# Gates of the GLA branch: from a plain product and a one-group unit to one seven-product unit of two groups

## The chip, the cores and the metric

The kernel runs on one core of a Trainium2 chip. The metric is the device time of one execution in microseconds (us), the median of several runs. The profile is that of one execution; TensorE is PE (its weight loads PEld), VectorE DVE, ScalarE ACT, GpSimd POOL, SyncE SP.

## The reference

The kernel computes one decoder layer in float32, for 512 tokens of width 1024. Only the token mixer matters here:

```
h = layer_norm(x)
q_g, k_g, v_g, r_g, a_lr, q_lat, kv_lat, gate_logits = split(h @ w_in)   # widths 512, 512, 1024, 1024, 16, 384, 320, 2048
o_gla = gla_chunked(q_g, k_g, v_g, log_sigmoid(a_lr @ w_gla_a2 + b) / 16)  # 4 heads
y_gla = (rms_norm(o_gla) * silu(r_g)) @ w_o_gla
y_mla = mla_attention(q_lat, kv_lat) @ w_o_mla
g_gla, g_mla = split(sigmoid(gate_logits + b_gate))                       # 1024 columns each
mix   = (g_gla * y_gla + g_mla * y_mla) @ w_out
h = layer_norm(alpha * h + mix);  out = layer_norm(alpha * h + square(relu(h @ w_ff1)) @ w_ff2)
```

The change concerns the product that makes the 1024 logits of g_gla, and work earlier in the kernel that prepares operands for it.

## The kernel before

**Products in three parts.** Each float32 operand is split into a high and a low half (`split`: ScalarE writes hi, L111, VectorE writes lo = x - hi, L112), and a product is three matmuls: hi by hi, hi by lo, lo by hi. In a product with the weights as the stationary operand these are L245, L246 and L247 (`gemm_fm`, moving tiles of 512 tokens); with the activations stationary, L279 to L281 (`gemm_tm`); in the product of r, L728 to L730 (`proj_r`); in the seven-product units, L1157 to L1159 (`unit`, moving tiles of 256 tokens). PSUM has two pools of four banks, pm (`MM`) and px (`PX`).

**Weights.** `plan` lists all weight tiles in the order of their use in one stream. `pump(i)` fetches two tiles ahead (on SP) and splits one tile ahead (hi on ScalarE at L189, lo on VectorE at L190), in three buffers of raw weights (wraw) and two each of hi and lo (whi, wlo).

**Seven products.** A product of 2 x 2 blocks is done with seven block products in place of eight, by Strassen's method in Winograd's form. Three of the products (11, 21, 22) use blocks of the weights as they are, and four (t1, t2, t3, t4) use sums of blocks: t1 is the load of block 12 on SP with an accumulating load of block 11 on POOL's queue (`u_load`, L1132 and L1134), t3 likewise with 22, and t2 and t4 follow from t1 and t2 by VectorE sums (`u_sum`, L356). The activations need the matching sums of h's blocks. `h_early` makes these for four pairs of k tiles: hraw (L1046) is hi plus lo of a tile again, hx (L1050 to L1053) are four sums and differences, and the halves of each are split into hs and written to DRAM as hsd (L1060). They are read back twice: by `proj_r` (xr) and, ahead of the gates, by `h_load` into sh (L1216). `proj_r` and three units use this form: g0 and g1 for the gates and f1 for a part of the first MLP product. A unit with two groups has two column groups of 512 output channels each, and so two sets of banks.

**The work around the change.** The product of q (from about 45 us) and of k are plain. Then come v of the first two heads, r, and v of the other two (to about 217 us), and beside them the decay levels of GLA: `gla_levels` copies the cumulated log decays of a head into rp (L766), POOL advances them by powers of two (L775, L776), ScalarE takes the exponentials E (L781), VectorE multiplies them by q and k into M (L783), and TensorE multiplies M by itself (L837, L841, L845). `gla_out` multiplies the scores by v (L880 to L882), squares (osq, L884), sums (gss, L887), takes the root on POOL (grs, L889), scales (og, L894) and transposes on TensorE (L900). From 217.90 us the gates of the first 512 channels of g_gla are a plain product (`gemm_fm` of `PL["g", 0]`), and then the other 512 channels are unit g0 with one group. Unit g1, with two groups, makes the 1024 channels of g_mla. Where a helper makes work in pieces, the pieces are co-routines: `spawn` puts one in a list, and `tick` lets the first few do a step each, between matmuls.

**The order.** The program is recorded in this way, and a scheduler then orders the instructions of each engine by a simulated timeline before the program runs. The order on each engine is fixed from then on. `tc.issue_after` holds one instruction behind another in it.

Of the kernel before, what the change touches and what calls it, by code (L numbers as in the profile page):

```python
# [52 lines left out]
def tile_hybrid_block(ctx: ExitStack, tc: tile.TileContext, I, out, dbg=None):  # L53
# [29 lines left out]
    def DR(shape, n):  # L83
        n = nm(n)
        return pd.tile(shape, F32, tag=n, name=n)
# [7 lines left out]
    def f(ap):  # L93
        return ap.bitcast(F32)
# [137 lines left out]
    def part(x, i, c):  # L232
        return x[i][:, c] if isinstance(x, tuple) else x[:, i, c]
# [94 lines left out]
    def plan_qr(g):  # L328
        PL["qr", g] = plan("w_q_b", NOPE, 4 * ROPE, heads=(HQ, 4 * g, 4))

    PL["g", 0] = plan("w_in", C_G, T)

    HOME = {"w": ("whi", "wlo"), "r": ("wraw", "wraw"), "a": ("xh", "xl")}
    FMO = (("11", 0), ("21", 1), ("t1", 2), ("22", 5), ("t2", 3), ("t3", 6), ("t4", 4))
    HELD = (("21", "f1"), ("21", "g0"), ("22", "g0"))
    ORDER = {"g0": ("11", "t1", "21", "t2", "22", "t3", "t4")}
    UNITS = {"g0": ("w_in", C_G + T, 1), "g1": ("w_in", C_G + D, 2), "f1": ("w_ff1", 3 * D, 2)}

    def plan_src(key, seq, homes):
        PL[key] = []  # L340
# [356 lines left out]
    def proj_r():  # L697
        bank, e, xs = {}, {}, {}

        def x_load(ph):  # L700
            xs[ph] = []
            for p in range(4):
                t = B([P, 2, 256], F32R, "xr")
                nc.sync.dma_start(f(t), hsd[p][(2, 3, 5, 6).index(ph)])
                xs[ph].append((t[:, 0], t[:, 1]))

        nat = {0: (0, 0), 1: (1, 0), 4: (1, 1)}
        for n, (op, ph) in enumerate(RW):
            if n + 1 < len(RW) and RW[n + 1][1] not in nat:
                x_load(RW[n + 1][1])  # L710
            if ph in nat:
                i, h = nat[ph]
                x = [tuple(hT[2 * p + i][:, w, 256 * h:256 * h + 256] for w in range(2)) for p in range(4)]
            else:
                x = xs.pop(ph)
            opens = ph in (0, 1, 2)
            for hf in range(2):
                it = PL["r"][2 * n + hf]
                pump(it)
                hi, lo = stream[it]["w"]  # L720
                for pp in range(2):
                    xh, xl = x[2 * hf + pp]
                    for t in range(2):
                        key = ("a" if ph in (0, 3, 6, 4) else "b", t)
                        if ph in (0, 1) and not hf and not pp:
                            bank[key] = MM()
                        o, c = bank[key], slice(t * P, (t + 1) * P)
                        mm(o, xh[:, c], hi[:, pp], start=opens and not hf and not pp, stop=False, skip_group_check=True)  # L728
                        mm(o, xh[:, c], lo[:, pp], start=False, stop=False, skip_group_check=True)
                        mm(o, xl[:, c], hi[:, pp], start=False, stop=hf == 1 and pp == 1, skip_group_check=True)  # L730
                    if (hf, pp) in RT:
                        tick(None)
            for t in range(2):
                a, b = bank["a", t], bank.get(("b", t))
                if ph in (0, 3, 2):
                    e[ph, t] = B([P, T], F32, "er")
                    act(e[ph, t], b if ph == 2 else a, AF.Copy)
                elif ph == 1:
                    vtt(e[0, t], b, e[0, t], op=ALU.add)
                    silu(0, t, e[0, t])  # L740
                elif ph == 6:
                    vtt(e[2, t], e[2, t], a, op=ALU.subtract)
                    silu(1, 2 + t, e[2, t])
                elif ph == 5:
                    vtt(e[3, t], b, e[3, t], op=ALU.subtract)
                    silu(1, t, e[3, t])
                else:
                    silu(0, 2 + t, a)
            if op == RA4:
                r_acc4()  # L750
# [11 lines left out]
    def gla_levels(h):  # L762
        qk = QK[h]
        QK[h] = None
        rp = A([P, 2, T], F32, "rp")
        nc.vector.tensor_copy(rp[:, 1, :], GL[h])  # L766
        nc.gpsimd.memset(rp[:, 0, :], 0.0)
        SD = B([P, NT, P], F32, "SD")
        SDf = SD.rearrange("p t i -> p (t i)")
# [267 lines left out]
    hsd = []  # L1037

    def h_early():
        for _ in range(6):  # L1040
            yield
        for p in range(4):
            raw = [B([P, T], F32, "hraw") for _ in range(2)]
            for i in range(2):
                h = hT[2 * p + i]
                vtt(raw[i], f(h[:, 0]), f(h[:, 1]), op=ALU.add)  # L1046
            yield
            a11, a12, a21, a22 = raw[0][:, :256], raw[1][:, :256], raw[0][:, 256:], raw[1][:, 256:]
            X = [B([P, 2, 256], F32, "hx") for _ in range(2)]
            vtt(X[0][:, 0], a21, a22, op=ALU.subtract)  # L1050
            vtt(X[0][:, 1], X[0][:, 0], a11, op=ALU.subtract)
            vtt(X[1][:, 0], a12, X[0][:, 1], op=ALU.add)
            vtt(X[1][:, 1], a11, a21, op=ALU.subtract)  # L1053
            yield
            hsd.append([DR([P, 2, 256], "hsd") for _ in range(4)])
            for i, x in enumerate(X):
                xs = [B([P, 2, 256], F32R, "hs") for _ in range(2)]
                for e in range(2):
                    split(x[:, e], xs[e][:, 0], xs[e][:, 1])
                    nc.sync.dma_start(hsd[p][2 * i + e], f(xs[e]))  # L1060
                yield

    t_ln1 = spawn(ln_in1())
# [72 lines left out]
    def unit(key, ops, evac, after=None, pb=None):  # L1136

        bank, e1, e5, u2 = {}, {}, {}, {}

        def prod(op):  # L1140
            ph = dict(FMO)[op]
            opens = ph in (0, 2, 1)
            for g in range(UNITS[key][2]):
                bk = ("a" if ph in (0, 3, 6, 4) else "b" if ph in (2, 5) else "c", g)
                if opens:
                    bank[bk] = (PX if ph == 1 else (pb or MM) if ph == 2 else MM)()
                o, it = bank[bk], PL[key, op, g]
                pump(it)
                hi, lo = stream[it]["w"]
                for k in range(4):  # L1150
                    while len(ops) <= k:
                        tick(3)
                    xh, xl = ops[k][ph]
                    for a in range(2):
                        c = slice(a * P, (a + 1) * P)
                        oa = o[:, a * 256:(a + 1) * 256]
                        mm(oa, hi[:, k, c], xh, start=opens and k == 0 and a == 0, stop=False, skip_group_check=True)  # L1157
                        mm(oa, hi[:, k, c], xl, start=False, stop=False, skip_group_check=True)  # L1158
                        mm(oa, lo[:, k, c], xh, start=False, stop=k == 3, skip_group_check=True)  # L1159
                    if k == 3 or k == 1 and key != "g0":  # L1160
                        tick(3)
                if ph == 0:
                    e1[g] = B([P, T], F32, "e1")
                    act(e1[g], o, AF.Copy)
                elif ph == 1:
                    vtt(e1[g], o, e1[g], op=ALU.add)
                    evac(0, 0, g, e1[g], True)
                elif ph == 2:
                    e5[g] = B([P, T], F32, "e5")
                    act(e5[g], o, AF.Copy)  # L1170
                elif ph == 3:
                    u2[g] = B([P, T], F32, "u2")
                    act(u2[g], o, AF.Copy)
                if ph == (5 if key == "g0" else 3):
                    vtt(u2[g], bank["b", g], u2[g], op=ALU.subtract)
                    evac(1, 0, g, u2[g], True)
                if ph == 6:
                    vtt(e5[g], e5[g], o, op=ALU.subtract)
                    evac(1, 1, g, e5[g], True)
                elif ph == 4:  # L1180
                    evac(0, 1, g, o, False)
            if after:
                after(op)
        return prod
# [17 lines left out]

    def ev_gate0(j, i, g, ps, _):
        for a in range(2):
            gate(0, 4 + 2 * j + a, ps[:, a * 256:(a + 1) * 256], slice(256 * i, 256 * i + 256))

    hops = []

    def h_load():
        for p in range(4):  # L1210
            o = {0: (0, 0), 1: (1, 0), 4: (1, 1)}
            o = {ph: tuple(part(hT[2 * p + i], w, slice(256 * h, 256 * h + 256)) for w in range(2))
                 for ph, (i, h) in o.items()}
            for x, ph in enumerate((2, 3, 5, 6)):
                t = B([P, 2, 256], F32R, "sh")
                nc.sync.dma_start(f(t), hsd[p][x])  # L1216
                o[ph] = (t[:, 0], t[:, 1])
            hops.append(o)
            yield

    spawn(h_load())
    u_load("g0", "t1")
    u_load("g0", "22")
    gemm_fm(PL["g", 0], hT, T, lambda a, ps: gate(0, a, ps, slice(0, T)))
    def after0(op):
        if op == "11":
            for o in ("t3", "21"):
# [400 lines left out]
```

## Time and profile before

| | |
|---|---|
| median of 3 runs | 891.93 us (891.44 to 892.49) |
| the profiled execution | 891.75 us, span 890.0 us |
| granted TensorE clock | 0.998 |
| PE busy | 871.3 us (98%) |
| PEld busy | 757.1 us (85%) |
| DVE busy | 634.6 us (71%) |
| ACT busy | 467.0 us (52%) |
| POOL busy | 186.8 us (21%) |

The span runs from the first to the last instruction of the profile, and the profiled execution's own time lies 1.75 us around it. Busy times count each engine's own instructions, and engines overlap. A matmul is drawn until its modelled end, so it overlaps its successor: the pitch from start to start tells its cost on TensorE. In timelines the columns are start, duration, engine, line, operation, output from inputs, sizes, and the number of instructions that are drawn together; a bracket gives idle time of the engine before the instruction and who ended it. In groups they are the count, busy time and mean in ns, and the idle time before. In rows of DMA the last number is the median time in us from issue to landing.

### The profile page before, as it was taken

To read this page: it belongs to the slowest core of one execution; us is meant where nothing else is said; L and a number is where in the kernel's file an instruction comes from. 1 tells how busy PE (TensorE), PEld (TensorE's weight loads), DVE (VectorE), ACT (ScalarE), POOL (GpSimd) and SP (SyncE) were. 2 spreads that over 40 slices of the span, in tenths; PEclk is the share of its full clock that TensorE was granted. 3 is DMA by queue.
4 is the path that set the end of the run, shared out by engine and by line. 5 is a ranking of instruction groups with operands and counts; after the bars stand their busy time and mean duration, and the time that the engine had idled before them with its cause. 6 is when DMAs were issued, how large, how long until landed. Compare 5 with 4: busy or idle time off the path is not lost.

```text
span 890.0 us, 12974 instructions
## 1 busy us (share of the span) xinstructions
PE 871.3 (98%) x4844; PEld 757.1 (85%) x4844; DVE 634.6 (71%) x1022; ACT 467.0 (52%) x828; POOL 186.8 (21%) x202
## 2 busy tenths in 40 slices
PE   5999999999999999999999999999999999999996
PEld 5988888888899988888888888988888888889985
DVE  7837999977366745657756797887556556788865
ACT  5557656655365643535644424466457546656810
POOL 0325547636021010100000003004400520141001
PEclk9999999999999999999999999999999999999999
DMA  7994738223879433111307518005950991399312
GB/s 236 284 227 150 275 121 236 95 75 109 279 177 241 133 101 101 42 54 54 103 16 284 190 50 305 1 1 138 305 124 14 264 250 41 80 230 234 119 61 82
DMA packets 86367, 130.92 MB, mean 147 GB/s; under 512 B 8945, under 2 KB 46705, under 8 KB 86305
## 3 DMA queue, kind: packets, MB, share of 16 engines
q1 hardware_dynamic: 67072, 91.83, 32.0%
q0 software_dynamic: 17312, 34.61, 18.1%
q10 hardware_dynamic: 1920, 3.66, 1.1%
q8 instruction: 38, 0.62, 0.3%
q14 instruction: 25, 0.20, 0.1%
HBM read 108.58 MB, written 8.91 MB: 132 GB/s over the span
## 4 chain that ended last, share of the span: by engine, by line
PE 89%; DVE 6%; issue 2%; ACT 1%; POOL 1%; DMA 1%; POOLq 0%; DVEq 0%; SPq 0%
PE mm L245 12%; PE mm L247 12%; PE mm L246 12%; PE mm L281 5%; PE mm L280 5%; PE mm L279 5%; PE mm L1159 3%; PE mm L1158 3%; PE mm L1157 3%; PE px L1441 2%; PE px L1439 2%; PE px L1440 2%; PE mm L1441 2%; PE mm L1439 2%; PE mm L1440 2%
## 5 line engine op out<-in xcount | busy, mean ns | idle before, releaser
L190 DVE TENSOR_TENSOR wlo<-wraw,whi 128x1024 fp32r<-128x1024 f32 (+2 forms) x93 | 102.5, 1102 | 102.9 <-ACT whi L189 98.5
L189 ACT ACTIVATE whi<-wraw 128x1024 fp32r<-128x1024 f32 (+2 forms) x93 | 88.5, 952 | 93.1 <-PE mm L246 44.8
L245 PE MATMUL mm<-h,whi 128*128 128x512 f32 x256 | 100.2, 392 | 0.0
L246 PE MATMUL mm<-h,whi 128*128 128x512 f32 x256 | 99.7, 389 | 0.0
L247 PE MATMUL mm<-h,wlo 128*128 128x512 f32 x256 | 96.0, 389 | 0.0
L1458 POOL DMA_DIRECT2D res<-ev x42 | 37.7, 1041 | 178.5 <-ACT ev L1456 143.8
L190 DVE TENSOR_TENSOR wlo<-wq,whi 128x1024 fp32r<-128x1024 f32 x44 | 55.3, 1256 | 25.2 <-ACT whi L189 25.2
L189 ACT ACTIVATE whi<-wq 128x1024 fp32r<-128x1024 f32 x44 | 46.5, 1056 | 24.9 <-PE mm L1158 11.9
L247 PEld LDWEIGHTS mm<-h,wlo 128*128 128x128 f32 x256 | 48.0, 188 | 10.1
L245 PEld LDWEIGHTS mm<-h,whi 128*128 128x128 f32 x256 | 48.1, 188 | 9.7
L246 PEld LDWEIGHTS mm<-h,whi 128*128 128x128 f32 x256 | 48.1, 188 | 9.7
L1159 PE MATMUL mm<-sh,wlo 128*128 128x256 f32 x160 | 45.4, 284 | 0.0
L1157 PE MATMUL mm<-sh,whi 128*128 128x256 f32 x160 | 45.4, 284 | 0.0
L1158 PE MATMUL mm<-sh,whi 128*128 128x256 f32 x160 | 45.3, 283 | 0.0
L189 ACT ACTIVATE xh<-wraw 128x1024 fp32r<-128x1024 f32 (+1 forms) x28 | 27.1, 982 | 28.6 <-PE mm L281 16.2
L428 POOL TENSOR_TENSOR mv<-mv,mhalf 128x1 f32<-128x1 f32 x4 | 3.3, 838 | 170.0 <-DVE mv L427 170.0
L190 DVE TENSOR_TENSOR xl<-wraw,xh 128x1024 fp32r<-128x1024 f32 (+1 forms) x28 | 31.3, 1128 | 8.5 <-ACT xh L189 8.5
L775 POOL TENSOR_TENSOR rp<-rp 128x256 f32<-128x256 f32 x32 | 31.5, 983 | 25.8 <-ACT E L781 14.4
L781 ACT ACTIVATE E<-rp 128x256 f32<-128x256 f32 x64 | 25.5, 416 | 20.1 <-POOL rp L776 11.1
L1501 ACT ACTIVATE relu<-mm 128x512 f32<-128x512 f32 x24 | 14.1, 596 | 41.3 <-PE mm L247 41.3
L776 POOL TENSOR_TENSOR rp<-rp 128x256 f32<-128x256 f32 x32 | 31.7, 989 | 8.7 <-ACT q L806 5.9
L783 DVE TENSOR_TENSOR M<-E,qk 128x512 f32<-128x512 f32 x32 | 29.5, 925 | 3.3 <-ACT E L781 3.3
(454 smaller groups left out, 2739.5 us busy)
## 6 DMA issues: line engine op xcount, KB each, us to landing
wraw<-in_w_ff_dram SPq DMA_DIRECT2D x36, 512.0 KB, 5.1
wraw<-in_w_in_dram SPq DMA_DIRECT2D x33, 512.0 KB, 4.1
wq<-in_w_ff_dram POOLq DMA_DIRECT2D x26, 512.0 KB, 9.6
res<-ev POOLq DMA_DIRECT2D x42, 256.0 KB, 9.9
wq<-in_w_in_dram SPq DMA_DIRECT2D x16, 512.0 KB, 6.3
wq<-in_w_in_dram POOLq DMA_DIRECT2D x16, 512.0 KB, 9.4
hsd<-hs SPq DMA_DIRECT2D x16, 256.0 KB, 2.6
xr<-hsd SPq DMA_DIRECT2D x16, 256.0 KB, 4.6
```

Source lines behind the costliest of these rows:

```text
L189: st["ins"] = act(hi[:, :nk, :n], raw[:, :nk, :n], AF.Copy)
L190: st["lo"] = vtt(lo[:, :nk, :n], raw[:, :nk, :n], f(hi[:, :nk, :n]), op=ALU.subtract)
L245: mm(o, hi[:, c], xh, start=first, stop=False)
L246: mm(o, hi[:, c], xl, start=False, stop=False)
L247: mm(o, lo[:, c], xh, start=False, stop=last)
L279: mm(o, xh, hi[:, :n], start=opens, stop=False, skip_group_check=share)
L280: mm(o, xh, lo[:, :n], start=False, stop=False, skip_group_check=share)
L281: mm(o, xl, hi[:, :n], start=False, stop=last, skip_group_check=share)
L1157: mm(oa, hi[:, k, c], xh, start=opens and k == 0 and a == 0, stop=False, skip_group_check=True)
L1158: mm(oa, hi[:, k, c], xl, start=False, stop=False, skip_group_check=True)
L1159: mm(oa, lo[:, k, c], xh, start=False, stop=k == 3, skip_group_check=True)
L1458: nc.gpsimd.dma_start(res[tt + t][:, j * T:(j + 1) * T], e, accum_op=ALU.add)
```

## The change

Three things are edited.

- The gates of g_gla become one unit of two groups from the first of their columns, and the plain product goes. Its order of products becomes 11, t1, t2, 22, t3, 21, t4, in which product 21 takes over bank b after it has been read, in place of a bank of its own. A product may begin when the operand of its own phase is loaded: `h_load` now loads phase by phase, four tiles each.
- The sums for the seven-product operands begin with the product of q (no steps are skipped), all four pairs are summed before the first is split, and a split and its store cover two sums (512 columns) at a time. The array hsd has another layout, and its two readers follow it.
- The copy into rp (L766) goes from VectorE to ScalarE.

```diff
--- before.py
+++ after.py
@@ -328,13 +328,12 @@
     def plan_qr(g):
         PL["qr", g] = plan("w_q_b", NOPE, 4 * ROPE, heads=(HQ, 4 * g, 4))
 
-    PL["g", 0] = plan("w_in", C_G, T)
 
     HOME = {"w": ("whi", "wlo"), "r": ("wraw", "wraw"), "a": ("xh", "xl")}
     FMO = (("11", 0), ("21", 1), ("t1", 2), ("22", 5), ("t2", 3), ("t3", 6), ("t4", 4))
     HELD = (("21", "f1"), ("21", "g0"), ("22", "g0"))
-    ORDER = {"g0": ("11", "t1", "21", "t2", "22", "t3", "t4")}
-    UNITS = {"g0": ("w_in", C_G + T, 1), "g1": ("w_in", C_G + D, 2), "f1": ("w_ff1", 3 * D, 2)}
+    ORDER = {"g0": ("11", "t1", "t2", "22", "t3", "21", "t4")}
+    UNITS = {"g0": ("w_in", C_G, 2), "g1": ("w_in", C_G + D, 2), "f1": ("w_ff1", 3 * D, 2)}
 
     def plan_src(key, seq, homes):
         PL[key] = []
@@ -701,7 +700,8 @@
             xs[ph] = []
             for p in range(4):
                 t = B([P, 2, 256], F32R, "xr")
-                nc.sync.dma_start(f(t), hsd[p][(2, 3, 5, 6).index(ph)])
+                x = (2, 3, 5, 6).index(ph)
+                nc.sync.dma_start(f(t), hsd[p][x // 2][:, x % 2])
                 xs[ph].append((t[:, 0], t[:, 1]))
 
         nat = {0: (0, 0), 1: (1, 0), 4: (1, 1)}
@@ -763,7 +763,7 @@
         qk = QK[h]
         QK[h] = None
         rp = A([P, 2, T], F32, "rp")
-        nc.vector.tensor_copy(rp[:, 1, :], GL[h])
+        act(rp[:, 1, :], GL[h], AF.Copy)
         nc.gpsimd.memset(rp[:, 0, :], 0.0)
         SD = B([P, NT, P], F32, "SD")
         SDf = SD.rearrange("p t i -> p (t i)")
@@ -1037,27 +1037,31 @@
     hsd = []
 
     def h_early():
-        for _ in range(6):
-            yield
+        for _ in range(0):
+            yield
+        Xs = []
         for p in range(4):
             raw = [B([P, T], F32, "hraw") for _ in range(2)]
             for i in range(2):
                 h = hT[2 * p + i]
                 vtt(raw[i], f(h[:, 0]), f(h[:, 1]), op=ALU.add)
-            yield
             a11, a12, a21, a22 = raw[0][:, :256], raw[1][:, :256], raw[0][:, 256:], raw[1][:, 256:]
             X = [B([P, 2, 256], F32, "hx") for _ in range(2)]
             vtt(X[0][:, 0], a21, a22, op=ALU.subtract)
             vtt(X[0][:, 1], X[0][:, 0], a11, op=ALU.subtract)
             vtt(X[1][:, 0], a12, X[0][:, 1], op=ALU.add)
             vtt(X[1][:, 1], a11, a21, op=ALU.subtract)
-            yield
-            hsd.append([DR([P, 2, 256], "hsd") for _ in range(4)])
-            for i, x in enumerate(X):
+            Xs.append(X)
+            yield
+        for _ in range(5):
+            yield
+        for p, X in enumerate(Xs):
+            hsd.append([DR([P, 2, 2, 256], "hsd") for _ in range(2)])
+            for d, x in zip(hsd[p], X):
                 xs = [B([P, 2, 256], F32R, "hs") for _ in range(2)]
-                for e in range(2):
-                    split(x[:, e], xs[e][:, 0], xs[e][:, 1])
-                    nc.sync.dma_start(hsd[p][2 * i + e], f(xs[e]))
+                split(x, *xs)
+                for w in range(2):
+                    nc.sync.dma_start(d[:, :, w], f(xs[w]))
                 yield
 
     t_ln1 = spawn(ln_in1())
@@ -1142,13 +1146,15 @@
             opens = ph in (0, 2, 1)
             for g in range(UNITS[key][2]):
                 bk = ("a" if ph in (0, 3, 6, 4) else "b" if ph in (2, 5) else "c", g)
-                if opens:
+                if ph == 1 and key == "g0":
+                    bank[bk] = bank["b", g]
+                elif opens:
                     bank[bk] = (PX if ph == 1 else (pb or MM) if ph == 2 else MM)()
                 o, it = bank[bk], PL[key, op, g]
                 pump(it)
                 hi, lo = stream[it]["w"]
                 for k in range(4):
-                    while len(ops) <= k:
+                    while len(ops) <= k or ph not in ops[k]:
                         tick(3)
                     xh, xl = ops[k][ph]
                     for a in range(2):
@@ -1202,26 +1208,25 @@
 
     def ev_gate0(j, i, g, ps, _):
         for a in range(2):
-            gate(0, 4 + 2 * j + a, ps[:, a * 256:(a + 1) * 256], slice(256 * i, 256 * i + 256))
+            gate(0, 4 * j + 2 * g + a, ps[:, a * 256:(a + 1) * 256], slice(256 * i, 256 * i + 256))
 
     hops = []
 
     def h_load():
         for p in range(4):
             o = {0: (0, 0), 1: (1, 0), 4: (1, 1)}
-            o = {ph: tuple(part(hT[2 * p + i], w, slice(256 * h, 256 * h + 256)) for w in range(2))
-                 for ph, (i, h) in o.items()}
-            for x, ph in enumerate((2, 3, 5, 6)):
+            hops.append({ph: tuple(part(hT[2 * p + i], w, slice(256 * h, 256 * h + 256)) for w in range(2))
+                         for ph, (i, h) in o.items()})
+        for x, ph in enumerate((2, 3, 5, 6)):
+            for p in range(4):
                 t = B([P, 2, 256], F32R, "sh")
-                nc.sync.dma_start(f(t), hsd[p][x])
-                o[ph] = (t[:, 0], t[:, 1])
-            hops.append(o)
+                nc.sync.dma_start(f(t), hsd[p][x // 2][:, x % 2])
+                hops[p][ph] = (t[:, 0], t[:, 1])
             yield
 
     spawn(h_load())
     u_load("g0", "t1")
     u_load("g0", "22")
-    gemm_fm(PL["g", 0], hT, T, lambda a, ps: gate(0, a, ps, slice(0, T)))
     def after0(op):
         if op == "11":
             for o in ("t3", "21"):
```

## The prediction

> **What bounds the kernel now.** I read the page first (busy shares, then the chain of work that ended last), then busy time by stretch, and then the timeline of TensorE, VectorE and GpSimd around the places that the change touches.
>
> ```profile
> span 890.0 us, 12974 instructions
> PE 871.3 (98%) x4844; PEld 757.1 (85%) x4844; DVE 634.6 (71%) x1022; ACT 467.0 (52%) x828; POOL 186.8 (21%) x202
> PE 89%; DVE 6%; issue 2%; ACT 1%; POOL 1%; DMA 1%; POOLq 0%; DVEq 0%; SPq 0%
> ```
>
> TensorE is the bound: 98% busy, 89% of the chain. A saving must therefore be TensorE work or a TensorE wait. The 6% of VectorE in the chain lies in one place, which the stretches show.
>
> ```profile
> 45.00:60.00 15.00, 15.00 (x74) 12.66 (x73) 4.27 (x6) 4.74 (x7) 4.94 (x5) 1.00 1.11 238
> 60.00:75.00 15.00, 15.00 (x68) 12.39 (x67) 9.31 (x11) 14.86 (x29) 6.28 (x4) 1.00 0.47 125
> ...
> 90.00:195.00 105.00, 103.22 (x552) 85.71 (x551) 97.50 (x162) 63.44 (x134) 60.05 (x64) 1.00 0.51 161
> 285.00:300.00 15.00, 15.00 (x128) 15.00 (x127) 11.26 (x10) 7.72 (x11) 0.00 (x0) 1.00 0.66 145
> ```
>
> The columns are the window, its length, and the busy time of PE, PEld, DVE, ACT and POOL, then clock and DMA. From 90 to 195 us (projections of v and r, with the decay levels of the GLA branch beside them) VectorE is busy 97.5 of 105 us, and TensorE shows 1.78 us of idle time. From 45 to 75 us (product of q) VectorE is busy only 13.6 of 30 us. From 285 us the existing seven-product unit of two groups (g1) runs with TensorE full, VectorE at 75% and the clock at 1.00. The gates in question start at 217.90 us, which I call T0:
>
> ```profile
> 217.90 0.40 PE L245 MATMUL mm<-h,whi 128*128 128x512 f32 x1
> ...
> 224.20 0.61 PE L841 MATMUL px<-M 128*128 128x128 f32 x4
> 224.56 0.36 PE L881 MATMUL px<-vl,s 128*128 128x256 f32 x1
> ```
>
> The idle of the second stretch is drawn too small, because a matmul is drawn longer than its pitch. Starts tell it better:
>
> ```profile
> 110.17 0.40 PE L279 MATMUL mm<-whi,h 128*128 128x512 f32 x1
> 111.01 0.41 PE L837 MATMUL px<-M 128*128 128x64 f32 x2 [0.44 <-DVE M L783]
> ...
> 120.98 0.40 PE L281 MATMUL mm<-whi,h 128*128 128x512 f32 x1
> 121.80 0.46 PE L841 MATMUL px<-M 128*128 128x128 f32 x2 [0.42 <-DVE M L783]
> ...
> 148.54 0.39 PE L730 MATMUL mm<-whi,xr 128*128 128x512 f32 x1
> 149.19 0.65 PE L837 MATMUL px<-M 128*64 128x64 f32 x8 [0.26 <-DVE M L783]
> 149.76 0.73 PE L728 MATMUL mm<-whi,xr 128*128 128x512 f32 x2
> 150.65 0.50 PE L729 MATMUL mm<-wlo,xr 128*128 128x512 f32 x1 [0.16 <-DVE wlo L190]
> ...
> 172.90 0.61 PE L837 MATMUL px<-M 128*128 128x64 f32 x4
> 173.83 0.50 PE L729 MATMUL mm<-wlo,h 128*128 128x512 f32 x1 [0.32 <-DVE wlo L190]
> ```
>
> **Part 1, TensorE work.** Two runs of matmuls without a stall give the pitch of each width:
>
> ```profile
> 228.63 0.39 PE L247 MATMUL mm<-h,wlo 128*128 128x512 f32 x1
> ...
> 231.35 0.39 PE L247 MATMUL mm<-h,wlo 128*128 128x512 f32 x1
> ```
>
> ```profile
> 284.01 0.28 PE L1157 MATMUL mm<-sh,whi 128*128 128x256 f32 x1
> ...
> 290.85 0.28 PE L1157 MATMUL mm<-sh,whi 128*128 128x256 f32 x1
> ```
>
> Twelve matmuls of 512 columns take 2.72 us, a pitch of 0.227 us; 57 of 256 columns take 6.84 us, a pitch of 0.120. The change removes the plain product of the first four gate tiles, 8 x 4 x 3 = 96 matmuls of 512 columns, 21.8 us, and adds a second group to the unit, 7 x 4 x 2 x 3 = 168 matmuls of 256 columns, 20.2 us. All of it is on the bound: minus 1.6 us. The gain is small because each narrow matmul carries more fixed time than half a wide one. [...]
>
> With the wide gemm its four weight splits go, and seven of the new group come. The order of instructions shows that from the end of this unit on every engine's order is as before, but for one swap of two matmuls near the second norm. So the effects are local: 45 to 262 us.
>
> **Part 2, VectorE between 90 and 195 us.** The operand sums and their splits move ahead, two splits of 256 columns become one of 512, and the copy into rp goes to ScalarE.
>
> ```profile
> L1046 DVE TENSOR_TENSOR hraw<-h 128x512 f32<-128x512 f32 x8 | 5.6, 736 | 0.0
> L1050 DVE TENSOR_TENSOR hx<-hraw,hraw 128x256 f32<-128x256 f32 x4 | 3.4, 856 | 0.0
> L112 DVE TENSOR_TENSOR hs<-hx,hs 128x256 fp32r<-128x256 f32 x16 | 8.5, 563 | 0.0
> L766 DVE COPY rp<-g 128x512 f32<-128x512 f32 x4 | 3.5, 870 | 0.0
> L111 ACT ACTIVATE sh<-hx x8: 612/625/636, 787.1 to 803.6; 128x512 fp32r<-128x512 f32 x8
> L112 DVE TENSOR_TENSOR sh<-hx,sh x8: 681/682/684, 790.1 to 804.5; 128x512 fp32r<-128x512 f32 x8
> ```
>
> The first four rows group busy time over 45 to 195 us; the last two are one existing split of 512 columns. In the order of before, two of the four pairs of operands have their sums, and ten of the 16 splits fall, behind 90 us. What leaves the full stretch is about half the sums (hraw half of 5.6; hx four kinds of about 0.42 to 0.86 us, two of four each, some 5), ten splits of 0.56 against perhaps three of 0.68 left there (minus 3.6), and 3.5 of copies: some 14 us of 97.5. In the quiet stretch from 45 us there are 16 us free, and there the splits of the weights come once in 24 matmuls (24 x 0.227 = 5.4 us), so the added 0.7 us pieces are covered; uncovered, one late split would cost up to 0.7 us.
>
> What it is worth is bounded by the five waits quoted, start to start less the pitch: 0.61, 0.59, 0.42, then 0.44 (0.89 less two of 0.227) and 0.64 (0.93 less four of L837 at 0.07, by its eight in the 0.57 from 149.19), together 2.7 us. They hold 1.60 of the 1.78 us of drawn idle, so by the same ratio all of it is 3.0: the ceiling. The floor is below nothing (minus 0.5, if the changed order puts a level's matmuls too early). The first two (1.2 us) lie where splits and sums stand before the waited-for M; I take them whole. The other three are behind splits of r's weights, which stay; two thirds of 1.5, for an engine with 14 us less to do. Together minus 2.2 us.
>
> **Part 3, the start of the unit.** Before, 21.8 us of plain product stood ahead of the unit, and the sums of weights and the loads of operands landed under it. Now the first product (11) is the only cover. T1 of both groups is a load on SP and an accumulating load on POOL:
>
> ```profile
> 218.11 1.34 POOL L1134 DMA_DIRECT2D wq<-in_w_in_dram  x1
> 219.12 0.99 POOL L775 TENSOR_TENSOR rp<-rp 128x256 f32<-128x256 f32 x1
> ...
> 225.24 1.02 PE L845 MATMUL px<-M 128*128 128x256 f32 x4
> 225.50 0.38 ACT L884 ACTIVATE osq<-px 128x256 f32<-128x256 f32 x1 [3.91 <-PE px L882]
> ...
> 227.54 1.65 DVE L894 SCALAR_TENSOR_TENSOR og<-px,grs,rg 128x256 f32<-128x256 f32 x4
> ...
> 231.58 0.38 PE L900 MATMUL px<-ca,og 128*128 128x128 f32 x2
> ```
>
> ```profile
> wq<-in_w_in_dram POOLq DMA_DIRECT2D x6, 512.0 KB, 7.7
> L189 ACT ACTIVATE whi<-wraw 128x1024 fp32r<-128x1024 f32 x19 | 20.1, 1056 | 18.5 <-PE mm L246 13.6 <-issue 2.7 <-PE mm L730 1.9
> L356 DVE TENSOR_TENSOR wq<-wq,wq 128x1024 f32<-128x1024 f32 x4 | 4.9, 1225 | 0.1
> ```
>
> Two things come late. First, the order now places the eight transposes of a GLA head (L900) only ten matmuls and L845 behind the head's last L882. The chain from there is osq, gss, grs, og: in the rows og's first quarter is ready near 228.0, 2.9 us behind the L882 that starts 0.12 before 225.24, and the last at 229.2. Work between: 0.12 + 10 x 0.12 + 0.7 for L845 = 2.0. So TensorE waits 0.9 us and, through the later quarters, some 0.35 more: 1.25. Before, wide matmuls filled that gap until 231.58. Second, the accumulating load of the second group is issued behind the GLA update L775, near 220.1 (219.12 + 0.99); with 7.7 us from issue to landing (the first of these rows, six such loads between 205 and 300 us) it lands at 227.8, and one hi split of 1.06 us (a weight split of that width) has it ready at 228.9. TensorE arrives at T0 + 48 x 0.12, plus the GLA head's matmuls that the order places between (15 x 0.12, L841 at 0.36, L845 at 0.68, eight transposes taken at 0.36 for four: 3.6), plus the 1.25 just told and two matmuls of the first group, at 228.7. Wait: 0.2. Who waits behind it: that hi split stands on ScalarE ahead of the head's ogT, e1 and osq, so a late landing holds these too. The second products are covered: T2 is summed on VectorE (1.2 us each) while 48 matmuls run. Later in the unit each buffer of split weights turns over in 24 x 0.12 = 2.88 us, as in g1, which is full in the row from 285 us. The bank b that the product 21 takes over is read out one whole product (5.8 us) earlier, and g1's first product waits for that read with 24 matmuls between: nothing. Bounds for part 3: 0 (the schedule is early enough elsewhere) to 5; I take plus 1.45, near the low end because the rows give it.
>
> **Sum.** The profiled execution took 891.75 (span 890.0 and 1.75 around it), 0.18 under the median of the three runs. 891.75 - 1.63 - 2.2 + 1.45 = 889.4.
>
> **Rivals.** *Order, not load* (0.25): the waits on M and wlo belong to matmuls placed too early in a fixed order, and the lighter VectorE only moves them; POOL and ScalarE pace the levels (POOL 60 us in the same stretch). For it: TensorE's places for the levels hardly move. Against it: VectorE names every one of the five waits. Then part 2 gives 0.4, and the time is 891.75 - 1.63 - 0.4 + 1.45 = 891.2, within what can be told from no change. *All of it* (0.14): every VectorE wait goes (3.0) and T1 is early, with half the og wait: 891.75 - 1.63 - 3.0 + 0.6 = 887.7. *T1 too late, slower* (0.17): the accumulating load shares the DMA engines with one 512 KB weight load and eight 256 KB operand loads issued in the same 6 us. The median of such loads over the whole kernel is higher:
>
> ```profile
> wq<-in_w_in_dram POOLq DMA_DIRECT2D x16, 512.0 KB, 9.4
> ```
>
> A landing x us after issue makes a wait of x - 7.7 + 0.2, and ScalarE's queue is held with it. At 9.4 that is 1.9. With part 2 at nothing the gain is gone from 7.9 us on, and the time is slower by more than can be told from no change (1.8 us, below) from 9.7; with part 2 whole these are 10.1 and 11.9. My price is a landing of 12 us with part 2 at 0.4: 891.75 - 1.63 - 0.4 + 1.25 + 4.5 = 895.5; twice the 7.7 would make it 898.9. [...] *Not what it says*: the instruction counts follow the diff, so no chance is set aside.
>
> **How the numbers follow.** Forecast 889.4 (0.44; its own range 888.3 to 890.5), order 0.25, all of it 0.14, too late 0.17. A measurement of this kernel tells about 0.2%, 1.8 us, from no change: faster means under 889.97. From the forecast's case some 0.34 and from the third 0.14, 0.03 from the second: 0.51. Slower means over 893.5: of the last case 0.14, of the second 0.03 (an order that costs more than it saves), 0.17. Within: 0.32. The range 887.2 to 894.0 takes in the forecast, the order case and the price of all of it, and leaves out most of the last case and the best of the third.
>
> **What would show it.** TensorE's count up by 72 (168 less 96), no waits of 0.5 us named after VectorE before L837 and L841 between 105 and 125 us, hraw and hx all before 80 us, L766 on ACT at about 0.6 us; VectorE's share of 90 to 195 us near 85%. Wrong would be: a wait of over 2 us at the first T1 matmuls, a gap before L900, or the waits on M and wlo in place at 149 and 174 us with VectorE no longer full.

## The result, and the profile after

The changed kernel is slower: 899.98 us (median of 4 runs, 899.06 to 902.06) against 891.83 (4 runs, 891.44 to 892.49), a ratio of 1.0098 over the runs with a 95% interval of 1.0085 to 1.0110 (the two medians alone give 1.0091). The forecast was 889.4, with a range of 887.2 to 894.0. The profiled execution took 899.06 with a span of 897.0; it is the fastest of the four, and the others show a lower mean clock (0.993 to 0.995 against 0.997).

First the page of the changed kernel: the span, the busy times, and the engines' shares of the chain that ended last.

```profile
span 897.0 us, 13130 instructions
PE 872.0 (97%) x4916; PEld 760.4 (85%) x4916; DVE 640.0 (71%) x1018; ACT 474.4 (53%) x834; POOL 186.6 (21%) x204
PE 89%; DVE 3%; DMA 2%; ACT 2%; POOL 1%; issue 1%; POOLq 0%; DVEq 0%; ACTq 0%
```

TensorE has its 72 matmuls more, as forecast. VectorE's share of the chain fell from 6% to 3%, and those of DMA and of ScalarE rose from 1% to 2% each. The timeline of TensorE at the beginning and the end of the gates, and at q, says in which stretch the 7.0 us of span lie (the last row is the first matmul behind both units).

```profile
46.53 0.39 PE L245 MATMUL mm<-h,whi 128*128 128x512 f32 x1
...
217.37 0.28 PE L1163 MATMUL mm<-h,whi 128*128 128x256 f32 x1
...
319.88 0.40 PE L279 MATMUL mm<-whi,latT 128*128 128x256 f32 x2
```

```profile
47.38 0.39 PE L245 MATMUL mm<-h,whi 128*128 128x512 f32 x1
...
312.81 0.40 PE L279 MATMUL mm<-whi,latT 128*128 128x256 f32 x2
```

The second fence is the same of the kernel before, whose gates began at 217.90. Up to q the changed kernel's profile is 0.85 us ahead, before anything that the change moves; in the traces of the other kernels of this case that row starts anywhere between 46.4 and 48.1 us. From q to the gates it took 170.84 us, before 170.52: plus 0.3, where part 2 of the prediction had minus 2.2. From the gates to the row behind both units it took 102.51 us, before 94.91: plus 7.6. Behind that it is equal (577.1 and 577.2). So the loss is in the unit. TensorE's timeline there (changed kernel) shows the wait:

```profile
225.01 1.03 PE L845 MATMUL px<-M 128*128 128x256 f32 x4
226.53 1.53 PE L900 MATMUL px<-ca,og 128*128 128x128 f32 x8 [0.48 <-DVE og L894]
227.81 0.36 PE L880 MATMUL px<-vh,sd 128*128 128x256 f32 x1
...
228.37 0.28 PE L1164 MATMUL mm<-sh,whi 128*128 128x256 f32 x1
233.11 0.58 PE L1163 MATMUL mm<-sh,whi 128*128 128x256 f32 x1 [4.46 <-ACT whi L189]
...
255.55 0.39 PE L1163 MATMUL mm<-sh,whi 128*128 128x256 f32 x1 [0.42 <-ACT whi L189]
255.77 0.28 PE L1164 MATMUL mm<-sh,whi 128*128 128x256 f32 x1
257.09 0.39 PE L1165 MATMUL mm<-sh,wlo 128*128 128x256 f32 x1 [1.04 <-DVE wlo L190]
```

Who held the hi split is one step further back, in the timelines of ScalarE and GpSimd:

```profile
219.31 1.05 POOL L775 TENSOR_TENSOR rp<-rp 128x256 f32<-128x256 f32 x1
220.31 1.29 POOL L1138 DMA_DIRECT2D wq<-in_w_in_dram  x1
```

```profile
232.00 1.06 ACT L189 ACTIVATE whi<-wq 128x1024 fp32r<-128x1024 f32 x1 [5.33 <-DMA wq<-in_w_in_dram]
```

The accumulating load of T1's second group was issued at 220.31 and landed 11.6 us later (at 231.92), ScalarE's queue stood behind it for 5.33 us, and TensorE for 4.62 (233.11 less 228.37 and one pitch of 0.12). And the matmuls behind the wait run at half the clock, which the busy time of that stretch shows in its third column from the end:

```profile
233.10:236.40 3.30, 3.29 (x15) 3.29 (x16) 3.30 (x4) 1.88 (x5) 0.00 (x0) 0.50 1.09 362
```

Fifteen matmuls take 3.37 us there where they would take 1.80: 1.57 us more. The sum of the stretch: matmuls minus 1.63, the gap before L900 and within it 1.40 (227.81 less 225.01, 0.68 and 0.72), the wait at T1 4.62, the half clock 1.57, the two waits near 256 us 1.99 with their tails (0.58 and 1.20): 7.95, against 7.60 measured. The 0.35 between them are not accounted for: in the stretch of before the matmuls stand without a gap but for one of 0.2 us.

### The profile page after: what moved, and what is told of

It is laid out like the page before. It is cut to its first block, busy times and chain, and to the rows that moved or that the text cites. A ratio compares the mean times of both kernels' runs of the same rounds, so it can differ in the third digit from the quotient of the medians.

```text
span 897.0 us, 13130 instructions
## 1 busy us (share of the span) xinstructions
PE 872.0 (97%) x4916; PEld 760.4 (85%) x4916; DVE 640.0 (71%) x1018; ACT 474.4 (53%) x834; POOL 186.6 (21%) x204
## 4 chain that ended last, share of the span: by engine, by line
PE 89%; DVE 3%; DMA 2%; ACT 2%; POOL 1%; issue 1%; POOLq 0%; DVEq 0%; ACTq 0%
PE mm L247 11%; PE mm L245 11%; PE mm L246 11%; PE mm L281 5%; PE mm L279 5%; PE mm L280 5%; PE mm L1165 4%; PE mm L1163 4%; PE mm L1164 4%; PE px L1446 2%; PE px L1445 2%; PE px L1444 2%; PE mm L1446 2%; PE mm L1445 2%; PE mm L1444 2%
## 5 line engine op out<-in xcount | busy, mean ns | idle before, releaser
L190 DVE TENSOR_TENSOR wlo<-wraw,whi 128x1024 fp32r<-128x1024 f32 (+1 forms) x90 | 101.1, 1124 | 89.7 <-ACT whi L189 85.2
L189 ACT ACTIVATE whi<-wraw 128x1024 fp32r<-128x1024 f32 (+1 forms) x90 | 85.4, 949 | 85.2 <-PE mm L246 39.1
L246 PE MATMUL mm<-h,whi 128*128 128x512 f32 x224 | 87.2, 389 | 0.0
L245 PE MATMUL mm<-h,whi 128*128 128x512 f32 x224 | 87.1, 390 | 0.0
L190 DVE TENSOR_TENSOR wlo<-wq,whi 128x1024 fp32r<-128x1024 f32 x50 | 61.7, 1233 | 34.1 <-ACT whi L189 34.0
L247 PE MATMUL mm<-h,wlo 128*128 128x512 f32 x224 | 83.5, 390 | 0.0
L1163 PE MATMUL mm<-sh,whi 128*128 128x256 f32 x192 | 55.1, 287 | 4.9 <-ACT whi L189 4.9
L1165 PE MATMUL mm<-sh,wlo 128*128 128x256 f32 x192 | 54.9, 287 | 1.0 <-DVE wlo L190 1.0
L1164 PE MATMUL mm<-sh,whi 128*128 128x256 f32 x192 | 54.9, 286 | 0.0
L246 PEld LDWEIGHTS mm<-h,whi 128*128 128x128 f32 x224 | 42.1, 188 | 8.8
L245 PEld LDWEIGHTS mm<-h,whi 128*128 128x128 f32 x224 | 42.1, 188 | 8.7
L1163 PEld LDWEIGHTS mm<-sh,whi 128*128 128x128 f32 x192 | 37.4, 195 | 5.3 <-ACT whi L189 5.3
L1165 PEld LDWEIGHTS mm<-sh,wlo 128*128 128x128 f32 x192 | 37.3, 195 | 1.2 <-DVE wlo L190 1.2
L1164 PEld LDWEIGHTS mm<-sh,whi 128*128 128x128 f32 x192 | 37.4, 195 | 0.0
```

The costliest lines, as they stand in the source:

```text
L189: st["ins"] = act(hi[:, :nk, :n], raw[:, :nk, :n], AF.Copy)
L190: st["lo"] = vtt(lo[:, :nk, :n], raw[:, :nk, :n], f(hi[:, :nk, :n]), op=ALU.subtract)
L245: mm(o, hi[:, c], xh, start=first, stop=False)
L246: mm(o, hi[:, c], xl, start=False, stop=False)
L247: mm(o, lo[:, c], xh, start=False, stop=last)
```

## The experiments

The theory was that T1's load lacks cover in the unit, and that the early sums give nothing. The rivals: the new layout of the sums makes the loads slow, or the DMA engines are simply full, so that any rearrangement only moves the wait.

**early_only: one half of the change.** The kernel before with the early sums, their layout and the rp copy; no edit to the gates.

> The kernel before with the early operand sums (with their splits, their array and its readers) and the rp copy on ScalarE, and no change to the gates. Theory now (the changed kernel took as long from the start of q to T0 as the one before, 170.8 against 170.5 us): no gain, 891.0 to 892.8 us. The prediction's part 2: minus 2.2, 889.6 us.

Measured 891.88 us against 891.87, ratio 1.0002 (0.9993 to 1.0011). The early sums with the rp copy are worth nothing that these runs can tell (0.1% either way), and they cost nothing.

**unit_only: the other half.** The kernel before with the unit of two groups alone.

> The kernel before with the gates as one unit of two groups (order, banks, phase-by-phase operand loads), and with the sums, splits and rp copy as before. Theory (the whole loss lies in the unit: the second T1 load lands late): 899 to 901 us, with a wait of 4 to 5 us at the first matmuls of T1. Rival (the new layout and early stores of the operand sums make the loads slow): 891 to 893 us and no such wait.

Measured 901.29 us, ratio 1.0104 (1.0090 to 1.0118). The same wait stands there (TensorE's timeline), so the layout and the early stores have no part in it:

```profile
229.18 0.28 PE L1159 MATMUL mm<-sh,whi 128*128 128x256 f32 x1
233.78 0.58 PE L1158 MATMUL mm<-sh,whi 128*128 128x256 f32 x1 [4.32 <-ACT whi L189]
```

**t1_early: T1's loads before the product of v.** The definition of `u_load` moves up with them.

```diff
+    u_load("g0", "t1")
     proj_v(1, lambda: levels_upto(1))
...
-    u_load("g0", "t1")
     u_load("g0", "22")
```

> The changed kernel with the loads of T1 (both groups, on SP and on POOL) recorded before the product of v of the last two heads, so that both land before the unit starts. Theory (the load is late because it is issued at 220 us in a crowded window): the 4.6 us wait and the slow matmuls behind it (1.6 us) go, 893.2 to 894.4 us; the waits of 1.4 us before L900 and 2.0 us near 256 us stay. Rival (the shared DMA engines are the limit, so what is issued earlier makes other loads late): the wait moves to another operand, 897 to 900 us.

Measured 895.94 us, ratio 1.0045 (1.0031 to 1.0058): the wait at T1 is gone, 4 us of the loss with it. The other 2 us did not come. The two waits behind product 22 stayed, and in the profiled execution the clock halved after those. Going by the mean clock that is most of what is missing: three of the four executions show a mean clock of 0.995 or 0.996 and took 895.92 to 896.45 us, and the one with 0.999 took 894.42.

```profile
250.76 0.28 PE L1166 MATMUL mm<-sh,wlo 128*128 128x256 f32 x1
251.47 0.39 PE L1164 MATMUL mm<-sh,whi 128*128 128x256 f32 x1 [0.42 <-ACT whi L189]
251.69 0.28 PE L1165 MATMUL mm<-sh,whi 128*128 128x256 f32 x1
253.01 0.48 PE L1166 MATMUL mm<-sh,wlo 128*128 128x256 f32 x1 [1.04 <-DVE wlo L190]
```

```profile
253.00:256.40 3.40, 3.39 (x16) 3.39 (x17) 1.97 (x3) 0.72 (x1) 1.24 (x1) 0.52 0.06 11
```

**t1_mid: one place on GpSimd's queue.** T1's loads (again with the definition of `u_load`) are recorded at the end of that product of v, so that the accumulating load stands before the GLA update L775 and not behind it.

```diff
-    proj_v(1, lambda: levels_upto(1))
+    proj_v(1, lambda: (levels_upto(1), u_load("g0", "t1")))
...
-    u_load("g0", "t1")
     u_load("g0", "22")
```

> The changed kernel with the loads of T1 recorded a little earlier, so that on GpSimd's queue the second accumulating load stands one place ahead, before the GLA update L775 and not behind it; it issues about 1 us sooner (219.3 us). Theory (issue time and shared engines): it lands 1 to 2 us earlier, the wait at T1 falls from 4.6 to 2.6 to 3.6 us, 897.5 to 899.2 us. Rival (it is behind the same operand loads anyway): it lands near 232 us and the time stays at 899.5 to 900.5 us.

Measured 893.23 us, ratio 1.0016 (1.0007 to 1.0025): 6.75 us less than the changed kernel, far more than either expectation. GpSimd's timeline, and then ScalarE's:

```profile
217.59 1.29 POOL L1109 DMA_DIRECT2D wq<-in_w_in_dram  x1
218.58 0.95 POOL L775 TENSOR_TENSOR rp<-rp 128x256 f32<-128x256 f32 x1
```

```profile
225.99 1.06 ACT L189 ACTIVATE whi<-wq 128x1024 fp32r<-128x1024 f32 x1 [0.28 <-PE mm L1164]
```

Of the 2.7 us by which it is issued earlier one is its place; the rest comes from the piece of POOL's work ahead of it (sd, L855), which began at 216.35 us here and at 218.04 in the changed kernel. The load took 7.4 us and landed 7.0 us earlier (224.95), and the split waits for no DMA. The changed kernel issued it behind the first of these of SP (its queue's timeline), here it went ahead of such loads:

```profile
218.17 0.37 SPq L174 DMA_DIRECT2D wraw<-in_w_in_dram  x1
218.58 0.51 SPq L1223 DMA_DIRECT2D sh<-hsd  x1
```

**quiet: fewer loads beside it.**

```diff
-        for x, ph in enumerate((2, 3, 5, 6)):
-            for p in range(4):
+        for p in range(4):
...
+            for ph in (2, 3, 5, 6):
...
-                u_load("g0", o)
+                for g in range(2):
+                    WQ["g0", (o, g)] = WQ["g0", ("22", g)]
```

> The changed kernel with fewer loads behind the accumulating load of T1: eight of twelve operand loads (phases 3, 5, 6 use the sums of phase 2) and the loads for t3 and 21 of the first unit (the weights of 22 stand in) are left out, so the gates are not the reference's. Theory (the DMA engines are shared): the second accumulating load of T1, 11.6 us from issue to landing in the changed kernel, takes 7 to 8.5 us, and the wait at T1 falls from 4.6 to under 1.5 us. Rival (the accumulating load takes that long by itself when it is the second on its queue): 11 to 12 us, and the wait stays. The total is 893 to 896 us by the first, since later loads go too; above 898 by the second.

Measured 891.23 us, ratio 0.9994 (0.9984 to 1.0004); the load, issued at 220.41, took 8.4 us, and no wait above 0.3 us is left at T1. The total fell below the expected 893: the waits near 256 us are gone too in this kernel, which doesn't load t3. DMA queues from the load's first packets to its landing: the changed kernel (221.6 to 231.9 us), quiet (221.7 to 228.8) and the kernel before (219.4 to 225.5); the columns are packets, MB, and share of the engines' time:

```profile
q1 hardware_dynamic: 1448, 2.60, 75.9%
q0 software_dynamic: 528, 0.52, 31.5%
```

```profile
q1 hardware_dynamic: 994, 1.42, 60.6%
q0 software_dynamic: 528, 0.52, 48.1%
```

```profile
q0 software_dynamic: 528, 0.52, 58.6%
q1 hardware_dynamic: 615, 0.70, 38.0%
```

It is the same load of 528 packets each time. Beside 0.70 MB on SP's queue it took 6.1 us, beside 1.42 MB 7.1, beside 2.60 MB 10.3. Share times length of the window gives what its own packets took of all 16 engines: 3.6, 3.4 and 3.2 us. For those of SP's queue it gives 2.3, 4.3 and 7.8 us. So the load's own work did not grow; the time in which the engines served SP's queue did. How the engines divide their time between the two queues these rows don't show.

**o21: more cover in place of an earlier load.** Product 21, whose weights are loaded as they are, comes second; it opens two banks that T1 takes over.

```diff
-    ORDER = {"g0": ("11", "t1", "t2", "22", "t3", "21", "t4")}
+    ORDER = {"g0": ("11", "21", "t1", "t2", "22", "t3", "t4")}
...
-                if ph == 1 and key == "g0":
-                    bank[bk] = bank["b", g]
+                if ph == 2 and key == "g0":
+                    bank[bk] = bank["c", g]
...
+    u_load("g0", "21")
     u_load("g0", "22")
```

> The changed kernel with another order of products, 11, 21, t1, t2, 22, t3, t4: product 21 opens two banks of the pm pool, is added to e1, and T1 takes these banks over; its weights are loaded ahead of 22. T1 then has 48 more matmuls (5.8 us) ahead of it. Theory (cover was missing): 4.6 us of wait and 1.6 us of slow matmuls go, 892.5 to 894.5 us. Rival (the DMA window): the two added loads of 512 KB make T1 later by about as much as it has more cover, 897 to 900 us.

Measured 890.06 us, ratio 0.9981 (0.9972 to 0.9990): faster than both kernels. Its accumulating loads are no faster (10.4 us each, landing at 224.05 and 229.65), but they are needed 5.8 us later, and eight transposes lie among the matmuls of 21 (TensorE's timeline):

```profile
217.53 0.28 PE L1163 MATMUL mm<-h,whi 128*128 128x256 f32 x1
...
229.15 1.03 PE L900 MATMUL px<-ca,og 128*128 128x128 f32 x8
...
310.73 0.40 PE L279 MATMUL mm<-whi,latT 128*128 128x256 f32 x2
```

From the gates to the row behind both units this is 93.20 us, 1.71 less than before, where part 1 said 1.63.

**o21_old and o21_rp: the early sums again, in a unit that doesn't wait.** The first has the sums and the rp copy of the kernel before, the second only the rp copy back on VectorE.

> The unit of two groups in the order 11, 21, t1, t2, 22, t3, t4, with the operand sums, their splits and the rp copy as in the kernel before. Theory (the early sums are worth nothing, the unit alone is worth the 1.6 us of matmuls): 889.6 to 890.8 us, as with the early sums (890.1). Rival (the early sums help once the unit no longer waits, for instance since their stores and loads are out of the way): 891.5 us or more.

> The order 11, 21, t1, t2, 22, t3, t4 with the early sums, and the rp copy back on VectorE. Theory (VectorE has room from 90 to 135 us since the sums left, so the copy costs nothing there, but of the waits of 1.1 and 0.5 us on M at 172 and 181 us it may lengthen one): 889.5 to 891 us. Rival (the copy on ScalarE delays POOL, whose kr comes 1.4 us later and makes TensorE wait 0.67 us at 105 us): 889.3 us or less.

Measured 889.78 (0.9979; 0.9970 to 0.9988) and 889.83 us (0.9979; 0.9970 to 0.9988), within the interval of o21. Neither the sums nor the engine of the copy makes a difference that these runs can tell.

**after_u: the waits near 256 us.** The read of bank b in the first unit is held behind the latest lo split.

```diff
-                    vtt(u2[g], bank["b", g], u2[g], op=ALU.subtract)
+                    with tc.issue_after(st["lo"].ins):
+                        vtt(u2[g], bank["b", g], u2[g], op=ALU.subtract)
```

> The changed kernel with one order edit: the subtraction that reads out bank b of the first unit (u2) is held behind the lo split recorded last, so that on VectorE the split of t3's weights no longer stands behind a read that waits for the last matmul of 22. Theory (the waits of 0.6 and 1.2 us at 255.5 and 257.1 us come from that place in VectorE's order): 1.2 to 2 us less than the changed kernel, 898 to 898.8 us. Rival (t3's accumulating load lands late, at 251.7 and 247.1 us, and the splits follow it): no change, 899.5 to 900.5 us.

Measured 899.78 us, ratio 1.0090 (1.0077 to 1.0104), as the changed kernel. The waits went from 0.58 and 1.20 to 0.58 and 0.92, which a wait at T1 of 5.45 us in its profiled execution outweighs. This theory fell: most of the waits is not from that place in VectorE's order. What paces that split is open; in t1_mid and t1_early the waits stand too, in quiet and o21 they don't.

**o21_m2 and o21_norg: what TensorE waits for from 145 to 185 us.** In the first, the four scalings of r (rg) are held behind the next M on VectorE; in the second ScalarE copies in their place, r stays unscaled, and VectorE has none of them. Their like without the edit is o21_rp.

> The order 11, 21, t1, t2, 22, t3, t4 with early sums and the rp copy on VectorE, and one order edit: the four scalings of r (rg, 3.2 us on VectorE) are held behind the next M instead of standing ahead of it. Theory (the waits of 1.19 us at 171.5 and 0.53 us at 180.4 us are the time that M stands behind this evacuation of r, which the early sums never touched): 1 us or more of these goes, 888.3 to 889.1 us against 889.8 without the edit. Rival (M is paced by the chain of E on ScalarE and rp on GpSimd, or another split takes its place): 889.5 to 890.2 us.

> As the kernel with order 11, 21, t1, ... , early sums and the rp copy on VectorE (889.8 us), but the scaling of r by its gate is left out: ScalarE copies the tanh into rg, so that 16 pieces of 0.8 us leave VectorE between 145 and 185 us. Theory (VectorE's own work at the evacuations of r, not the operand sums, is what M and wlo wait for at 149, 171 and 180 us, 2.2 us together): 1.2 to 2 us less, 887.8 to 888.6 us. Rival (the places of the matmuls in the fixed order and the chain of E and rp pace them): 889.3 us or more, with the waits still there.

The first took 890.93 us (0.9987; 0.9978 to 0.9996), no faster: the wait went to the M behind the scalings (1.48 us at 173.4). The second took 887.56 (0.9960; 0.9947 to 0.9974), by the ratios 1.7 us under its like (0.9979), though the two intervals still touch, and the three waits are gone. VectorE's and TensorE's timelines of the like, and then of this one:

```profile
167.12 3.20 DVE L674 SCALAR_TENSOR_TENSOR rg<-th,er 128x256 f32<-128x256 f32 x4
170.25 1.10 DVE L783 TENSOR_TENSOR M<-E,qk 128x512 f32<-128x512 f32 x1
171.49 1.89 PE L837 MATMUL px<-M 128*128 128x64 f32 x16 [1.02 <-DVE M L783]
```

```profile
169.63 0.69 DVE L782 TENSOR_TENSOR M<-E,qk 128x512 f32<-128x512 f32 x1 [0.19 <-ACT E L780]
171.24 0.39 PE L729 MATMUL mm<-whi,xr 128*128 128x512 f32 x1
171.47 0.78 PE L836 MATMUL px<-M 128*128 128x64 f32 x6
```

M is ready 1.0 us earlier (170.32 and 171.35), and TensorE no longer stands waiting for it. The fixed order differs here by one place only: 14 wide matmuls lie between this group on M and the one before it in the like, 13 in this kernel.

## Why the prediction was wrong

**Part 1 was right**: 1.63 us forecast, 1.71 in o21, where nothing else is in the way.

**Part 2 failed at "an engine with 14 us less to do".** The relief was 10.5 us, and it lies almost wholly in the first half. The pieces that were to leave did leave: their rows fell from 14.6 to 1.4 us between 90 and 195 us, while other work there took longer (twelve scalings of r 8.9 us in place of 7.1). Busy time by stretch, before, changed kernel and o21_norg (VectorE is the third busy time):

```profile
90.00:135.00 45.00, 44.14 (x233) 36.86 (x232) 44.04 (x83) 27.80 (x62) 23.99 (x29) 1.00 0.56 190
135.00:195.00 60.00, 59.09 (x320) 48.85 (x319) 53.46 (x80) 35.65 (x74) 36.06 (x36) 1.00 0.46 139
```

```profile
90.00:135.00 45.00, 44.35 (x239) 37.69 (x238) 34.96 (x65) 27.57 (x58) 25.42 (x29) 1.00 0.55 187
135.00:195.00 60.00, 58.19 (x313) 48.18 (x313) 52.09 (x77) 37.05 (x74) 34.09 (x37) 1.00 0.43 129
```

```profile
135.00:195.00 60.00, 59.90 (x325) 49.88 (x324) 46.36 (x63) 39.99 (x88) 36.96 (x36) 1.00 0.47 135
```

VectorE lost 9.1 us up to 135 us and 1.4 after. The two waits of the first half (111 and 122 us, 1.2 us) went, as forecast; a wait of 0.67 us for krh came at 105 us, and the three of the second half stayed or moved (0.58, 1.14 and 0.53 us at 148, 172 and 181 us). Averaging 90 to 195 us as one stretch hid this. That VectorE's load makes these waits was not wrong: with r's own scalings off VectorE there, all three waits went and 1.7 us came, and an edit to the order alone (o21_m2) only moved a wait. So the rival "order, not load" had the right price for part 2 (about nothing), but not the right reason.

**Part 3 failed at "with 7.7 us from issue to landing".** It was 11.6 us, and the wait behind it 4.62 us in place of 0.2. The issue came as forecast (220.31 for 220.1), and the transposes' gap was right (1.25 forecast, 1.40 measured). The 7.7 us were a median over six loads, and the one of them at the gates was issued at 218.11 us, ahead of SP's operand loads (SP's queue, kernel before):

```profile
219.70 9.15 SPq L1216 DMA_DIRECT2D sh<-hsd  x12
```

My own issue time for the second load, 220.1 us, lies behind that row's start: the nearest row had other neighbours. The rival "T1 too late" had the case (chance 0.17) with nearly the measured landing: 12 us priced, 11.6 measured, a wait of 4.5 priced, 4.62 measured. That the loads beside it make it late was right (8.4 us in quiet, from issue to landing); that the size fits is in part luck, since no row gave the 12 us. Its price of 895.5 was 4.5 us short of 899.98 and 3.6 short of the profiled execution's 899.06: the half clock (1.57) and the waits near 256 us (1.99) are in no step. "As in g1, which is full" was the argument against late splits there, and it does not hold for g0.

**What the runs put in its place.** With the load's wait taken away by order alone (t1_mid) the time is 893.2; with more cover (o21) it is 890.1, which is part 1's gain alone: that order has neither the gap before L900 nor the wait, and part 2 gives nothing.

## What to carry to other kernels

A transfer's time from issue to landing depended in these runs on what else was queued when it was issued (7.4 to 11.6 us for the same load): take it from a row with the same neighbours ahead of it, and check on every queue what the new order places in front. When cover is removed from the head of a stage, put the product that needs no prepared operand second, since here more work ahead of the wait (o21) helped although the load stayed slow. Read an engine's load in windows as short as the waits it is to explain.

## What the runs showed of the hardware

The granted clock was 0.50 over 233.10 to 236.40 us of the changed kernel, behind the wait of 4.62 us. In unit_only, behind a wait of 4.48 us (233.78 less 229.18 and one pitch), it was 0.50 over 233.80 to 237.10 us and 0.73 on average over the next 3.90 us. In t1_early it was 0.52 over 253.00 to 256.40 us, behind two waits of 0.59 and 1.20 us that ended at 251.47 and 253.01 us. Behind two such waits in the changed kernel, of 0.58 and 1.20 us, that ended at 255.55 and 257.09 us, it was 1.00 (busy time by stretch, with the clock in the third column from the end):

```profile
255.55:257.09 1.54, 0.50 (x2) 0.29 (x2) 1.49 (x2) 1.15 (x3) 0.00 (x0) 1.00 1.07 159
257.09:260.40 3.31, 3.31 (x28) 3.31 (x29) 2.26 (x4) 1.20 (x2) 0.00 (x0) 1.00 0.48 77
```

The two pairs differ by 0.01 us in their lengths, and the clock halved after the one and not after the other. The length of the waits alone thus doesn't tell what the clock does in these traces; what else decides it they don't show.
